# Wide matmuls for the high weights: one 512-column product over both parts of x, the halves added on eviction

## The chip, the cores and the metric

The kernel runs on one core of a Trainium2 chip. The metric is the device time of one execution in microseconds (us). It is told as the median of the timed runs. A profile of one execution with its trace goes with them.

The engines are called as in the profile: PE is TensorE's matmuls, PEld its weight loads, DVE is VectorE, ACT is ScalarE, POOL is GpSimd, SP is SyncE, which issues the DMAs.

## The reference, cut to what matters

256 tokens of 1024 features go through three layers. The first two are an mLSTM mixer and a gated spatial mixer, each followed by a feed-forward with a squared ReLU. The third is attention beside a convolution, then "PEER" experts, then a gated projection. Only two pieces of it matter here:

```python
y = jnp.square(jax.nn.relu(h @ ffn_w1[i])) @ ffn_w2[i]     # twice; w1 is 1024 x 4096

u = expert_u[et]                                           # peer: 16384 experts,
v = expert_v[et]                                           # 128 chosen per token
act = jax.nn.gelu(jnp.einsum('tnd,td->tn', u, xt)) * gt
return jnp.einsum('tn,tnd->td', act, v)
```

All of it is fp32, with seeded random inputs.

## The kernel before, in words

**Split products.** Every dense product is made of three matmuls in the fp32r type. ACT rounds an operand to a high part (`hi`, line 350, a cast), and DVE subtracts to get the rest (`lo`, line 351). The product is then hi times hi, hi times lo and lo times hi, summed in PSUM. Weights come in tiles of 1 MB (128 partitions x 2048 values). `weights` loads one and splits it into two tiles of 128x1024; the pool `wsp` has 4 buffers of `hi` and 4 of `lo`, so the cast for a tile reuses the buffer of the tile four places earlier and waits until PE has read that.

**Two forms of product.** In `dense_b` (line 392) the weights are the stationary operand and x, 256 tokens wide, is the moving one. One output tile is 128 outputs x 256 tokens and sums over k = 0 to 7, three matmuls of 256 columns for each k (`mm3`, lines 382 to 384): 24 matmuls and 24 weight loads. The tile lies in a PSUM buffer of the pool `mm`, which has two. In `Acc.emit` (line 113) x is stationary and the weights move, 512 columns in one matmul.

**Feed-forwards.** `ffn` (line 549) runs 16 steps n2. Each makes two tiles of the hidden layer with `pair`, which calls `dense_b`, except that the first tiles were already made ahead (`head`: 4 in the first feed-forward, 3 in the second). A tile is evicted by ACT (relu, line 565) and DVE (`s`, line 567, which reads PSUM and the relu), split into `h` and `l`, and one step later multiplied with `ffn_w2` in 24 matmuls of line 113. Between the steps `pump` lets side work run, here the conditioning rows `ada` (line 507, on DVE).

**Experts.** All 16384 experts are computed for all tokens in four quarters. `up(g)` (line 1142) makes the 32 tiles of a quarter in 16 steps b2 of two, each evicted by one ACT instruction (gelu, line 1147) from PSUM into `gx[g]`. `down(g)` multiplies `gx[g]` with the second matrix. The weight of an expert for a token is put in by `gate` (line 1150) in 32 steps of eight tokens for a set of quarters: DVE makes one-hot matrices `A`, `E` and `B` (lines 1159, 1161, 1164), PE multiplies them into a tile `sd` (line 1169 or 1180), and DVE multiplies `gx` with it. For quarter 0 (`wide`) ACT copies half of `sd` to `gs` (line 1171), DVE adds the other half (line 1172) and multiplies (line 1174); for the others DVE does it at once (line 1183). These steps are side work, taken from a budget after each step b2. The order is: route, gate(0) in the background of up(0), up(1), up(2); gate(1, 2) in the background of down(0), up(3); gate(3) in the background of down(1), down(2); down(3).

```python
            up(2, 3.0)
            self.drain()
            self.side = [gate((1, 2), iota2, op)]
            down(0, vp, 2.0)
            up(3, 4.0)
```

The budgets let two gate steps run per step b2 in up(2) and in up(3). Within each engine the instructions stand in a fixed order, which is set when the program is built; each engine works through its own in that order and waits on semaphores.

Of the kernel before, what the change touches and what calls it, by code (L numbers as in the profile page):

```python
# [10 lines left out]
F32 = mybir.dt.float32  # L11
F32R = mybir.dt.float32r
# [5 lines left out]
ALU = mybir.AluOpType  # L18
# [242 lines left out]
class Net:  # L261
# [129 lines left out]

    def dense_b(self, x, w, kc=KD, m=128, ps=None):

        (xh, xl), (wh, wl) = x, w
        if ps is None:
            ps = self.mm_tile()[:m, :T]
        for k in range(kc):
            last = self.mm3(ps, wh[:, k], wl[:, k], xh[:, k], xl[:, k], k == 0, k == kc - 1)
        self.flush(last)
        return ps  # L400

    def acc_tiles(self, n=1024):

# [27 lines left out]

        return [(ap[i][:, :1024 * min(2, n - 2 * i)], min(2, n - 2 * i), 128) for i in range((n + 1) // 2)]

    def pair(self, x, ap, i, first=0):

        have = min(2, max(0, len(self.head.ps) - first - 2 * i))
        ws = self.weights_b(ap[i][:, 1024 * have:]) if have < 2 else []
        for j in range(2):
            yield self.head.ps[first + 2 * i + j] if j < have else self.dense_b(x, ws[j - have])

    def h_tiles(self):
        return (self.hp.tile([128, KD, T], F32R, tag="hhi", name="hhi"),
                self.hp.tile([128, KD, T], F32R, tag="hlo", name="hlo"))

    def transpose_split(self, hi, lo, src, kc):

# [102 lines left out]
    def ffn(self, x, i, fin, pump=0.0):  # L549
        nc = self.nc  # L550
        w1, w2 = self.a["ffn_w1"], self.a["ffn_w2"]
        acc = Acc(self, 32, tail=6, fin=fin)
        with self.tc.tile_pool(name="ffn", bufs=6) as fp:
            pend = []

            def second():
                n2, parts = pend.pop(0)
                for p, w in zip(parts, self.weights(w2[i, n2])):
                    acc.add(p, w)

            for n2 in range(16):
                parts = []
                for ps in self.pair(x, w1[i], n2):
                    r = fp.tile([128, T], F32, tag="r", name="r", bufs=2)
                    nc.scalar.activation(r, ps, AF.Relu)
                    s = fp.tile([128, T], F32, tag="s", name="s", bufs=2)
                    nc.vector.scalar_tensor_tensor(s, ps, 0.0, r, op0=ALU.max, op1=ALU.mult)
                    h = fp.tile([128, T], F32R, tag="h", name="h")
                    l = fp.tile([128, T], F32R, tag="l", name="l")
                    self.split(h, l, s)  # L570
                    parts.append((h, l))
                pend.append((n2, parts))
                if 1 <= n2 < 14:
                    second()
                if 2 <= n2 < 13:
                    self.pump(pump)
                if n2 == 13:
                    self.drain()
            while pend:
                second()  # L580
        return fin.x
# [548 lines left out]
    def experts(self, x):  # L1130
        nc, a = self.nc, self.a
        with ExitStack() as es:
# [9 lines left out]
            def up(g, budget=0.0):  # L1142
                gx[g] = pools.get(g, gxa).tile([128, 32, T], F32, tag="gx", name="gx")
                for b2 in range(16):
                    for j, w in enumerate(self.weights_b(a["peer_u"][g * 16 + b2])):
                        ps = self.dense_b(x, w)
                        self.last = nc.scalar.activation(gx[g][:, 2 * b2 + j], ps, AF.Gelu_apprx_tanh)
                    self.pump(budget)

            def gate(groups, iota2, op, wide=False):  # L1150
# [4 lines left out]
                for t8 in range(T // 8):  # L1155
# [10 lines left out]
                    def apply_wide(ts=ts, A=A, B=B):  # L1166
                        pg = self.sd_tile().rearrange("p (t c j) -> p t c j", t=8, c=2)
                        for i in range(8):
                            nc.tensor.matmul(pg[:, i], A[:, i // 2, :, i % 2], B[:, :, i // 2, :, i % 2], start=True, stop=True)
                        s = op.tile([128, 8, 32], F32, tag="gs", name="gs")  # L1170
                        nc.scalar.copy(s, pg[:, :, 1])
                        nc.vector.tensor_tensor(s, s, pg[:, :, 0], op=ALU.add)
                        o = gx[groups[0]][:, :, ts]
# [332 lines left out]
```

## Time and profile before

| | |
|---|---|
| median of 3 timed runs | 1779.6 us (1777.91 to 1779.66) |
| the profiled execution: own time | 1777.44 us |
| its span in the trace | 1775.7 us |
| PE busy | 1727.9 us, 97% of the span, 11986 matmuls |
| PEld busy | 1545.4 us, 87% |
| DVE busy | 1370.4 us, 77% |
| ACT busy | 865.8 us, 49% |
| chain that ended last | PE 85%, DVE 7%, ACT 3%, DMA 2%, issue 2% |
| granted TensorE clock | 0.994 of full speed in the mean |
| moved by DMA | 352.51 MB, 199 GB/s in the mean |

The span runs from the first to the last instruction in the trace; the execution's own time has 1.7 us more around it. A matmul's busy time overlaps the next one's, so what a matmul costs in a stream is read from the distance of starts and not from its duration; the same holds, less strongly, for DVE and ACT. The shares are means over stages with different limits: the feed-forwards lie at about 176 to 365 us and 536 to 716 us of the span, up(0) to up(2) at about 975 to 1266, down(0) to 1362, up(3) to 1463, and the other down stages after it.

### The profile page before, as it was taken

What the parts mean: (1) busy time and instruction counts of PE and PEld (TensorE: products, weight loads), DVE (VectorE), ACT (ScalarE), POOL (GpSimd) and SP (SyncE); (2) the same over time, 40 slices, a digit from 0 to 9 for tenths busy, and PEclk for the clock granted to TensorE, in tenths of its full rate; (3) what the DMA queues carried; (4) which work ended last, traced back from release to release, by engine and by line L of the source; (5) the groups of instructions that cost most, each with busy time, mean ns of one, the idle gap of its engine ahead of it and who ended that gap; (6) DMA issues with size and microseconds to landing.
All of it is one profiled execution on the core that took longest, in us unless ns stands there. A gap on an engine that the chain in (4) does not pass through costs nothing.

```text
span 1775.7 us, 29680 instructions
## 1 busy us (share of the span) xinstructions
PE 1727.9 (97%) x11986; PEld 1545.4 (87%) x11986; DVE 1370.4 (77%) x2366; ACT 865.8 (49%) x1372; POOL 42.8 (2%) x50
## 2 busy tenths in 40 slices
PE   7999999999999999998999999999999999999998
PEld 3878889887879899898989999999988998888886
DVE  6687887579957655899867999789788958965654
ACT  3565445454545544564645445455444344444644
POOL 0110000000000000002000000000000000000000
PEclk9999999999999999999999999999999999999999
DMA  9874897467827653543436555544555454455751
GB/s 350 307 273 155 326 332 279 165 244 258 292 70 287 240 189 117 197 143 119 146 119 227 175 178 182 184 164 170 172 180 175 147 187 167 167 179 180 264 190 48
DMA packets 59604, 352.51 MB, mean 199 GB/s; under 512 B 6165, under 2 KB 12613, under 8 KB 19273
## 3 DMA queue, kind: packets, MB, share of 16 engines
q1 hardware_dynamic: 59466, 350.61, 56.1%
q8 instruction: 94, 1.54, 0.3%
q14 instruction: 44, 0.36, 0.1%
HBM read 349.51 MB, written 1.07 MB: 197 GB/s over the span
## 4 chain that ended last, share of the span: by engine, by line
PE 85%; DVE 7%; ACT 3%; DMA 2%; issue 2%; POOL 1%; SPq 0%; POOLq 0%; DVEq 0%; ACTq 0%
PE acc L113 38%; PE mm L382 13%; PE mm L384 13%; PE mm L383 13%; PE head L135 2%; DVE lo L351 2%; PE sd L1180 2%; DMA st<-in_ada_w_dram 1%; ACT hi L350 1%; DVE yc L894 1%; ACT junk L162 1%; DMA st<-in_a_w_v_dram 1%; DVE ada L507 1%; POOL rs_r L427 1%; PE sd L799 1%
## 5 line engine op out<-in xcount | busy, mean ns | idle before, releaser
L351 DVE TENSOR_TENSOR lo<-st,hi 128x1024 fp32r<-128x1024 f32 (+1 forms) x507 | 614.8, 1225 | 176.4 <-ACT hi L350 175.1
L350 ACT CAST hi<-st 128x1024 fp32r<-128x1024 f32 (+1 forms) x507 | 523.7, 1048 | 453.1 <-PE mm L383 225.2
L382 PE MATMUL mm<-hhi,hi 128*128 128x256 f32 (+1 forms) x2000 | 575.8, 288 | 0.7 <-ACT qz L629 0.7
L384 PE MATMUL mm<-hhi,lo 128*128 128x256 f32 (+1 forms) x2000 | 566.9, 284 | 8.0 <-DVE lo L351 7.9
L383 PE MATMUL mm<-hlo,hi 128*128 128x256 f32 (+1 forms) x2000 | 567.0, 284 | 0.0
L384 PEld LDWEIGHTS mm<-hhi,lo 128*128 128x128 f32 (+1 forms) x2000 | 383.7, 192 | 9.0 <-DVE lo L351 9.0
L382 PEld LDWEIGHTS mm<-hhi,hi 128*128 128x128 f32 (+1 forms) x2000 | 384.0, 192 | 3.6 <-issue 1.4
L383 PEld LDWEIGHTS mm<-hlo,hi 128*128 128x128 f32 (+1 forms) x2000 | 384.3, 192 | 3.1 <-issue 2.1
L113 PE MATMUL acc<-hi,vh 128*128 128x512 f32 x448 | 141.0, 396 | 0.0
L113 PE MATMUL acc<-lo,vh 128*128 128x512 f32 x448 | 138.3, 390 | 0.0
L113 PE MATMUL acc<-hi,vl 128*128 128x512 f32 x448 | 137.9, 389 | 0.0
L507 DVE SCALAR_TENSOR_TENSOR ada<-st,cact,ada 128x1024 f32<-128x1024 f32 x74 | 95.2, 1287 | 10.1 <-DMA st<-in_ada_w_dram 5.9
L113 PE MATMUL acc<-hi,h 128*128 128x512 f32 x320 | 100.5, 395 | 2.4 <-ACT hi L350 2.4
L113 PE MATMUL acc<-lo,h 128*128 128x512 f32 x320 | 100.4, 394 | 0.1
L113 PE MATMUL acc<-hi,l 128*128 128x512 f32 x320 | 99.9, 393 | 0.0
L113 PEld LDWEIGHTS acc<-hi,vl 128*128 128x128 f32 x448 | 84.1, 188 | 17.9
L113 PEld LDWEIGHTS acc<-lo,vh 128*128 128x128 f32 x448 | 84.1, 188 | 17.9
L113 PEld LDWEIGHTS acc<-hi,vh 128*128 128x128 f32 x448 | 81.6, 188 | 15.0
L350 ACT CAST vh<-gx 128x512 fp32r<-128x512 f32 x64 | 39.9, 624 | 96.2 <-PE acc L113 94.1
L113 PE MATMUL acc<-hi,hhi 128*128 128x512 f32 x224 | 73.6, 406 | 4.0 <-ACT hhi L350 2.1
L113 PE MATMUL acc<-lo,hhi 128*128 128x512 f32 x224 | 72.4, 396 | 1.0 <-DVE lo L351 0.9
L113 PEld LDWEIGHTS acc<-lo,h 128*128 128x128 f32 x320 | 60.3, 189 | 13.7 <-DVE lo L351 1.0
(380 smaller groups left out, 2174.8 us busy)
## 6 DMA issues: line engine op xcount, KB each, us to landing
st<-in_peer_u_dram SPq DMA_DIRECT2D x64, 1024.0 KB, 4.8
st<-in_peer_v_dram SPq DMA_DIRECT2D x64, 1024.0 KB, 4.8
st<-in_ffn_w_dram SPq DMA_DIRECT2D x63, 1024.0 KB, 4.9
st<-in_ada_w_dram SPq DMA_DIRECT2D x40, 1024.0 KB, 5.6
st<-in_ada_w_dram SPq DMA_DIRECT2D x16, 512.0 KB, 7.2
st<-in_b_w_u_dram SPq DMA_DIRECT2D x8, 1024.0 KB, 5.0
st<-in_b_w_v_dram SPq DMA_DIRECT2D x8, 1024.0 KB, 4.8
st<-in_b_w_out_dram SPq DMA_DIRECT2D x8, 1024.0 KB, 5.8
```

The source lines that it names most:

```text
L113: ins = mm(self.t[t][j], a[:, ts], b[:, j * 512:(j + 1) * 512], start=first and a is xh and b is wh, stop=last and a is xl)
L135: net.nc.tensor.matmul(ps[:, t * 128:(t + 1) * 128], w[:, k], x(k), start=k == 0, stop=k == KD - 1)
L162: nc.scalar.activation(net.junk[:, halves[h]], src, AF.Square, scale=1.0 / 32.0, accum_out=out[:, h:h + 1])
L350: i = self.nc.scalar.copy(hi, src)
L351: return i.ins, self.nc.vector.tensor_tensor(lo, src, hi.bitcast(F32), op=ALU.subtract).ins
L382: mm(out, ahi, bhi, start=start, stop=False)
L383: mm(out, ahi, blo, start=False, stop=False)
L384: return mm(out, alo, bhi, start=False, stop=stop)
L427: nc.gpsimd.tensor_tensor(r, v, m, op=ALU.pow)
L507: nc.vector.scalar_tensor_tensor(s, w, c, s, op0=ALU.mult, op1=ALU.add)
L799: nc.tensor.matmul(ps[:, t], v[:, t, n * 128:(n + 1) * 128], ws[:, n], start=False, stop=t == 1)
L1180: nc.tensor.matmul(pg[:, i], A[:, i // 2, :, i % 2], B[:, c, i // 2, :, i % 2], start=c == 0, stop=c == 1)
```

## The change

For the 57 hidden tiles of the feed-forwards that are not made ahead, and for the 64 tiles of up(2) and up(3), a new `dense_w` takes the place of `dense_b`. The two parts of x now lie side by side in one tile `h2` (`h_tiles`), so that one matmul of 512 columns multiplies the high weights with both. Each k has this one and a matmul of 256 columns for the low weights: 16 matmuls per tile where there were 24. The result fills a whole PSUM buffer of 512 columns, and its two halves must be added: `added` has ACT copy the second half to SBUF (`half`) and DVE add the first half to it. In the feed-forwards DVE then squares in a further instruction. In the experts the sum is written to `gx` and ACT's gelu runs on it in place.

```diff
     def dense_b(self, x, w, kc=KD, m=128, ps=None):
-        (xh, xl), (wh, wl) = x, w
+        xh, xl, (wh, wl) = x[0], x[1], w
...
+    def dense_w(self, x, w):
+
+        xh, x2, (wh, wl) = x[0], x[2], w
+        mm = self.nc.tensor.matmul
+        ps = self.mm_tile()
+        for k in range(KD):
+            first, last = k == 0, k == KD - 1
+            if last:
+                mm(ps[:, :T], wl[:, k], xh[:, k], start=False, stop=False)
+            i = mm(ps, wh[:, k], x2[:, k], start=first, stop=last)
+            if not last:
+                i = mm(ps[:, :T], wl[:, k], xh[:, k], start=False, stop=False)
+        self.flush(i)
+        return ps
+
+    def added(self, ps, out, pool, tag):
+
+        c = pool.tile([128, T], F32, tag=tag, name="half", bufs=2)
+        self.nc.scalar.copy(c, ps[:, T:])
+        self.nc.vector.tensor_tensor(out, ps[:, :T], c, op=ALU.add)
...
-    def pair(self, x, ap, i, first=0):
+    def pair(self, x, ap, i, first=0, wide=False):
...
-            yield self.head.ps[first + 2 * i + j] if j < have else self.dense_b(x, ws[j - have])
+            yield self.head.ps[first + 2 * i + j] if j < have else (self.dense_w if wide else self.dense_b)(x, ws[j - have])
 
     def h_tiles(self):
-        return (self.hp.tile([128, KD, T], F32R, tag="hhi", name="hhi"),
-                self.hp.tile([128, KD, T], F32R, tag="hlo", name="hlo"))
+
+        x = self.hp.tile([128, KD, 2, T], F32R, tag="h2", name="h2")
+        return x[:, :, 0], x[:, :, 1], x.rearrange("p k c t -> p k (c t)")
...
-                for ps in self.pair(x, w1[i], n2):
-                    r = fp.tile([128, T], F32, tag="r", name="r", bufs=2)
-                    nc.scalar.activation(r, ps, AF.Relu)
+                for ps in self.pair(x, w1[i], n2, wide=True):
                     s = fp.tile([128, T], F32, tag="s", name="s", bufs=2)
-                    nc.vector.scalar_tensor_tensor(s, ps, 0.0, r, op0=ALU.max, op1=ALU.mult)
+                    if ps.shape[1] == T:
+
+                        r = fp.tile([128, T], F32, tag="r", name="r", bufs=2)
+                        nc.scalar.activation(r, ps, AF.Relu)
+                        nc.vector.scalar_tensor_tensor(s, ps, 0.0, r, op0=ALU.max, op1=ALU.mult)
+                    else:
+                        self.added(ps, s, fp, "r")
+                        nc.vector.scalar_tensor_tensor(s, s, 0.0, s, op0=ALU.max, op1=ALU.mult)
...
-                        ps = self.dense_b(x, w)
-                        self.last = nc.scalar.activation(gx[g][:, 2 * b2 + j], ps, AF.Gelu_apprx_tanh)
+                        o = gx[g][:, 2 * b2 + j]
+                        if g < 2:
+                            ps = self.dense_b(x, w)
+                        else:
+
+                            ps = o
+                            self.added(self.dense_w(x, w), o, op, "gs")
+                        self.last = nc.scalar.activation(o, ps, AF.Gelu_apprx_tanh)
...
-                        s = op.tile([128, 8, 32], F32, tag="gs", name="gs")
+                        s = op.tile([128, T], F32, tag="gs", name="gs").rearrange("p (t j) -> p t j", t=8)
```

Where the new instructions stand in the engines' orders is shown at three places.

The first is DVE in the middle of up(2), one step b2 with its two gate steps. `lo` is the split of weights, `A`, `E`, `B`, `gs` and `gx<-gx,gs` are the gate's. Before:

```order
L1161 TENSOR_TENSOR E<-iota_8916,rT_8904 128x4x64 x2
L351 TENSOR_TENSOR lo<-st,hi 128x1024 x2
L1159 TENSOR_TENSOR A<-iota_8916,rT_8903 128x1024
L1164 TENSOR_TENSOR B<-E,gT 128x8x64
L1172 TENSOR_TENSOR gs<-gs,sd 128x256 x2
L1174 TENSOR_TENSOR gx<-gx,gs 128x32x8 x2
L1159 TENSOR_TENSOR A<-iota_8916,rT_8903 128x1024
L1164 TENSOR_TENSOR B<-E,gT 128x8x64
```

The same step with the change (lines are 33 further down):

```order
L1194 TENSOR_TENSOR E<-iota_8509,rT_8497 128x4x64 x2
L351 TENSOR_TENSOR lo<-st,hi 128x1024 x2
L1192 TENSOR_TENSOR A<-iota_8509,rT_8496 128x1024
L1197 TENSOR_TENSOR B<-E,gT 128x8x64
L1192 TENSOR_TENSOR A<-iota_8509,rT_8496 128x1024
L1205 TENSOR_TENSOR gs<-gs,sd 128x256 x2
L1207 TENSOR_TENSOR gx<-gx,gs 128x32x8 x2
L1197 TENSOR_TENSOR B<-E,gT 128x8x64
L421 TENSOR_TENSOR gx<-mm,half 128x256 x2
```

The two adds (line 421) stand together at the end of the step, behind the whole gate work of it.

The second is ACT at the end of up(2), after the last full pair of gate steps, with buffer numbers. `hi_12811` is the cast that reuses the buffer which the tile `mm_12713` reads; `half` are the new copies.

```order
L350 CAST hi_12807<-st_12805 128x1024
L1204 COPY gs_12692<-sd_12683 128x256
L1204 COPY gs_12705<-sd_12696 128x256
L350 CAST hi_12811<-st_12805 128x1024
L420 COPY half_12709<-mm_12666 128x256
L420 COPY half_12730<-mm_12713 128x256
```

The copy for `mm_12666` stands behind a cast that waits for the end of the next tile, `mm_12713`.

The third is PE in up(3), with buffer numbers, at the sixth of its steps b2.

```order
L411 MATMUL mm_14400<-h2_8438,hi_14392 128x512
L411 MATMUL mm_14459<-h2_8438,hi_14396 128x512
L413 MATMUL mm_14400<-h2_8438,lo_14393 128x256
L411 MATMUL mm_14400<-h2_8438,hi_14392 128x512
L413 MATMUL mm_14400<-h2_8438,lo_14393 128x256
```

The first matmul of the tile `mm_14459` now stands inside `mm_14400`, ahead of the matmuls that need `lo_14393`; it happens again two steps later. Outside the changed stages the order of PE, DVE, ACT and POOL is as before, and on SP one load changes places with its neighbours.

## Rows read from the trace of the kernel before

**Rows 1.** The page's first line.

```profile
span 1775.7 us, 29680 instructions
```

**Rows 2.** Chain that ended last, second feed-forward: start us, us, what.

```profile
570.90 5.47 PE acc L113 x24
582.12 5.47 PE acc L113 x24
```

**Rows 3.** Groups of instructions: count, busy, mean ns | idle, releaser.

```profile
L565 ACT ACTIVATE r<-mm 128x256 f32<-128x256 f32 x57 | 21.6, 380 | 47.6 <-PE mm L384 47.6
L1147 ACT ACTIVATE gx<-mm 128x256 f32<-128x256 f32 x128 | 48.7, 380 | 0.0
```

**Rows 4.** Busy time by stretch: us, PE, PEld, DVE, ACT, POOL, PEclk, DMA, GB/s.

```profile
187.00:330.00 143.00, 140.58 (x866) 125.02 (x866) 114.52 (x135) 70.94 (x101) 2.01 (x1) 0.99 0.81 298
536.00:705.00 169.00, 168.94 (x1059) 152.55 (x1058) 109.46 (x137) 82.44 (x127) 1.08 (x2) 1.00 0.60 214
1180.00:1240.00 60.00, 60.00 (x615) 59.57 (x615) 60.00 (x113) 30.39 (x58) 0.00 (x0) 1.00 0.47 159
1380.00:1412.00 32.00, 32.00 (x362) 31.83 (x360) 31.83 (x57) 11.98 (x18) 0.00 (x0) 1.00 0.47 163
```

**Rows 5.** Chain that ended last, a DVE chain on SBUF of 256 columns.

```profile
738.20 3.67 DVE yc L894 x10
```

**Rows 6.** Timeline of PE in the first feed-forward, around its longest wait.

```profile
198.27 0.28 PE L384 MATMUL mm<-hhi,lo 128*128 128x256 f32 x1
200.92 1.21 PE L113 MATMUL acc<-hi,h 128*128 128x512 f32 x4 [2.37 <-ACT hi L350]
...
203.18 1.06 PE L113 MATMUL acc<-hi,l 128*128 128x512 f32 x2
204.03 1.06 PE L113 MATMUL acc<-lo,h 128*128 128x512 f32 x2
```

**Rows 7.** Timeline of DVE in up(2), one step: start us, us, what.

```profile
1192.65 2.35 DVE L351 TENSOR_TENSOR lo<-st,hi 128x1024 fp32r<-128x1024 f32 x2
1194.92 0.68 DVE L1159 TENSOR_TENSOR A<-iota,rT 128x1024 f16<-128x1024 f16 x1
1195.52 0.42 DVE L1164 TENSOR_TENSOR B<-E,gT 128x512 f16<-128x512 f16 x1
1195.88 0.75 DVE L1172 TENSOR_TENSOR gs<-gs,sd 128x256 f32<-128x256 f32 x2
1196.54 1.17 DVE L1174 TENSOR_TENSOR gx<-gx,gs 128x256 f32<-128x256 f32 x2
1197.63 0.69 DVE L1159 TENSOR_TENSOR A<-iota,rT 128x1024 f16<-128x1024 f16 x1
1198.22 0.43 DVE L1164 TENSOR_TENSOR B<-E,gT 128x512 f16<-128x512 f16 x1
1198.56 0.50 DVE L1161 TENSOR_TENSOR E<-iota,rT 128x256 f16<-128x256 f16 x2
1198.96 2.36 DVE L351 TENSOR_TENSOR lo<-st,hi 128x1024 fp32r<-128x1024 f32 x2
```

**Rows 8.** Timeline of PE in up(2): the gate's matmuls between two of the tiles'.

```profile
1181.62 0.28 PE L384 MATMUL mm<-hhi,lo 128*128 128x256 f32 x1
1181.75 0.66 PE L1169 MATMUL sd<-B,A 128*128 128x64 f16 x16
1182.24 0.36 PE L382 MATMUL mm<-hhi,hi 128*128 128x256 f32 x1
```

**Rows 9.** Timeline of ACT in up(2).

```profile
1194.52 1.05 ACT L350 CAST hi<-st 128x1024 fp32r<-128x1024 f32 x1 [1.54 <-issue]
1195.48 0.64 ACT L1171 COPY gs<-sd 128x256 f32<-128x256 f32 x2
```

**Rows 10.** Timeline of DVE in up(3), the same instruction one step apart.

```profile
1385.54 1.41 DVE L1183 TENSOR_TENSOR gx<-gx,sd 128x256 f32<-128x256 f32 x4
1392.34 1.42 DVE L1183 TENSOR_TENSOR gx<-gx,sd 128x256 f32<-128x256 f32 x4
```

## The prediction

> **What bounds the kernel now.** I set the sum against the profiled execution: 1777.4 us, of which the span is 1775.7 [rows 1]. It lies 2.2 us below the median of 1779.6, so a time worked out here is raised by 2.2 at the end. No change, as far as a measurement of this kernel can tell, means within 0.2%, 3.55 us either way.
>
> First the chain that ended last: PE is 85% of it, so look at what a matmul costs in a stream. In the second feed-forward 24 matmuls of 512 columns stand in 5.47 us, 228 ns each. From one such group to the next are 11.22 us; the other 5.75 hold the 48 matmuls of 256 columns of two hidden tiles, 119.8 ns each [rows 2]. Twice the columns are not twice the time: at 2.4 GHz 256 columns are 106.7 ns and 512 are 213.3, so each matmul carries some 13 to 14 ns beyond its columns.
>
> Second the groups, for what ACT does per tile now: relu or gelu, 380 ns [rows 3].
>
> Third the busy time by stretch, which says who has room. In the feed-forwards PE fills nearly all of the time and DVE 114.5 of 143 us and 109.5 of 169. In the middle of up(2) PE and DVE are both busy for 60.00 of 60 us, in up(3) DVE for 31.83 of 32 [rows 4]. There any new DVE work meets an engine with no gap.
>
> **The saving on PE.** Per k, three matmuls of 256 columns (3 x 120 = 360 ns) become one of 512 and one of 256 (227 + 120 = 347): 13 ns, eight times per tile, 0.106 us. That is 57 x 0.106 = 6.1 us in the feed-forwards, 32 x 0.106 = 3.4 in each of up(2) and up(3), 12.9 in all if PE sets the pace everywhere.
>
> Beside that row the Trainium skill ("TensorE: Matmul & The Clock Gate", section "Wait — 56ns, not 53.3ns?") speaks against the change: it gives a fixed cost of only about 2.5 ns per matmul at the higher clock. By it the 968 matmuls that vanish would save an estimated 2.4 us. The rows disagree, with five times that.
>
> **Feed-forwards.** ACT's copy takes the place of its relu, both of 128x256 from PSUM, so ACT gains nothing [rows 3]. DVE gets one more instruction per tile, the square on SBUF. Ten dependent DVE instructions of 256 columns take 3.67 us, 0.37 each [rows 5], so 28 and 29 tiles add some 10.5 us each: 125 of 143 and 120 of 169 us [rows 4], which still fits. Per step a tile has two turns of 2.75 us before its buffer is needed; copy, add and square together take 1.1. So I cost these at nothing, covered by PE's own stream; without that cover each tile would pay about 0.37. What stays is the saving, 6.1 us, less where something else already ends the wait: in the first feed-forward PE waits 2.37 us for a cast of weights that come by DMA (the share of the DMA engines is 0.81 there), and faster matmuls only lengthen such a wait [rows 4, 6]. I take **-5.5**. Bounds: -6.1, and -2.3 if a third of the tiles lose it.
>
> **up(2).** One step b2 lies between two splits of weights, 1192.65 and 1198.96: 6.31 us, filled by DVE instruction to instruction [rows 7]. PE needs in it 48 x 0.12 = 5.76, and between two tile matmuls 0.62 us for the gate's 16, 0.50 above the normal distance [rows 8]: 6.26. The two engines are level. The change adds two adds of 256 columns from PSUM. The nearest row is the gate's own add of that form, two in 0.66 us start to start [rows 7]. So DVE needs 6.31 + 0.67 = 7.0 us and PE 6.26 - 0.21 = 6.05 to 6.1. PE has two buffers; the adds stand at the end of the step behind the whole gate work, so the tile after next waits there, 0.9 us per step. Twelve steps carry two gate steps. Through their order I get a first wait of 0.8, ten of 0.9, and at the end one longer: the copy for `mm_12666` stands behind the cast into the buffer that `mm_12713` reads. So that tile ends, then cast 1.05 [rows 9], split 1.17 (half of 2.35) and add 0.33 [rows 7], 2.6 us. Together 12.4, less 16 x 0.21 = 3.4 for PE's saving: **+9.0**. ACT is busy for 30 of 60 us [rows 4], so two copies of 0.32 [rows 9] and a gelu on SBUF cost nothing themselves. Bounds: if the split of the next weights and E fill some of the waits, DVE alone sets 11 steps of 0.66 more against 5 of saving, +6.2; above, the hand-overs between copy, add and matmul add about 0.1 per step, +10.
>
> **up(3).** Here a step lasts 6.80 us [rows 10], of which PE's matmuls fill all and DVE all but a little [rows 4]. After the change DVE needs 6.68 + 0.67 = 7.35 and PE 6.80 - 0.21 = 6.59: 0.75 short in each of the seven steps with two gate steps, 5.3 us. DVE's lead over PE at the start takes 0.7 of it. The remaining 4.6 should show as three waits of about 0.9, 1.5 and 2.2, where the first matmul of a tile (`mm_14459`) now stands inside the tile ahead and holds the rest of that up. Less 3.4: **+1.2**. Bounds -1 and +4.
>
> **The clock.** After the idle 2.37 us at 198.5 us the 512-column matmuls stand 0.43 us apart instead of 0.23, which is 1.2 in place of 2.4 GHz [rows 6]. The half rate lasts some 3.4 us and so costs 1.7. The waits of 2.6 and 2.2 us that I expect at the end of up(2) and in up(3) are near 2.37; those of 0.9 are not. I count one such stretch, **+1.7**; bounds none and three.
>
> **Sum**: -5.5 + 9.0 + 1.2 + 1.7 = +6.4, 1783.8 against the own time of 1777.4, and 1786.0 against the median.
>
> **Rivals.**
>
> *The adds cancel the gain.* The floor in up(2) (+6.2), up(3) at -1, the full saving in the feed-forwards (-6.1) and no further drop of the clock: -0.9, 1778.7. For it speaks that DVE's instructions could be set closer once PE waits; against it that rows 7 show no gap to close. Chance 0.2.
>
> *PE sets the pace everywhere, faster.* If DVE found 0.86 us per step in up(2), the 0.66 of the adds and the 0.21 that PE gains, all 121 tiles keep their saving: -12.9, 1766.7. It decides at that point, and the 60.00 of 60 speak against it [rows 4]; shorter DVE instructions while PE idles would speak for it. Chance 0.08.
>
> *It is dearer.* If the `ada` rows on DVE in the feed-forwards leave no room for the square in their steps, some 15 of the 28 steps lose their 0.21 (3.2 us), and if two more waits end at half clock (3.4), the sum is +13.0, 1792.6. The DVE share of 80% in the first feed-forward allows it, but it is a mean [rows 4]. Chance 0.12.
>
> *The merge saves almost nothing on PE.* If a matmul of 512 columns right beside one of 256 paid its weight load in full, so that the pair took 358 instead of 347 ns, the saving would shrink to a fifth, +10.4 on the sum, about 1797. In rows 2 the streams of 512 and 256 are each unmixed, so this isn't excluded, but no row speaks for it. Chance 0.02. The skill's 2.5 ns, named above, would give a similar time.
>
> **How the numbers follow.** Forecast, slower: 0.58, itself within 1783 to 1790 (feed-forwards -6.1 to -4, up(2) +8 to +10, up(3) 0 to +3, up to two stretches at half clock). Cancel 0.20, faster 0.08, dearer 0.12, no saving 0.02. The likeliest gives 1786.0. The range runs from 1778.0 (the cancel case in) to 1791.5 (half of the dearer case in); outside stay 0.08 + 0.02 + some 0.09 of the edges. Faster by over 0.2% is only the case of PE's pace, 0.08. Within 0.2%, up to 1783.2, is the cancel case and the lowest edge of the forecast, 0.22. Slower is the rest, 0.70.
>
> **What would show it.** In the feed-forwards the steps should shorten from 11.22 to about 11.0 us, with a 512-256 pair in 347 ns. In up(2) the steps with two gate steps should lengthen from 6.31 to about 7.0, with DVE full and PE waiting once per step for DVE's add; its other four steps shorten by 0.2. up(3) should hold two or three waits behind the add and the split. If PE's waits in up(2) are of another releaser, or if DVE's step stays at 6.3, the step that prices the adds is wrong. If the pair is not 347 ns, the saving is.

## The result and the profile after

The change made the kernel slower: 1798.2 us (1795.9 to 1799.7, 4 runs) against 1779.5 (1777.9 to 1779.7, 4 runs), a ratio of 1.0108, 95% interval [1.0093, 1.0122]. Forecast were 1786.0 and a range up to 1791.5. The sign was right, the size three times too small, and the time lies outside the range.

The page's first line; that of before is [rows 1].

```profile
span 1795.6 us, 27876 instructions
```

**Where the time went.** Both kernels make the same 716 casts to a high part on ACT, in nearly the same order, so the start of the same cast tells how far the one runs behind the other. From such marks (us of the span of before, and how much later the same cast starts after):

| cast of before starts at | 178 | 362 | 536 | 715 | 1014 | 1173 | 1287 | 1362 | 1468 | 1755 |
|---|---|---|---|---|---|---|---|---|---|---|
| after, later by | +2.7 | +0.9 | -0.6 | -2.7 | -1.9 | -1.8 | +15.5 | +15.5 | +19.6 | +19.6 |

The first feed-forward gained 1.8 us, the second 2.1, up(2) lost 17.3 and up(3) 4.1. The 1.5 us between the feed-forwards are a stretch at half clock that only the profile of before has there (granted clock 0.50 from 526.5 to 529.9 us). The 2.7 us ahead of the first feed-forward are taken up below. The busy time by stretch shows what changed in each; its columns are as in [rows 4], and so are its stretches:

```profile
187.00:330.00 143.00, 139.96 (x686) 116.08 (x685) 122.96 (x160) 71.05 (x101) 2.01 (x1) 0.99 0.82 305
536.00:705.00 169.00, 168.94 (x845) 142.33 (x845) 122.03 (x169) 85.30 (x130) 1.08 (x2) 1.00 0.61 213
1180.00:1240.00 60.00, 51.44 (x385) 42.72 (x384) 56.16 (x113) 31.25 (x64) 0.00 (x0) 1.00 0.42 141
1380.00:1412.00 32.00, 31.26 (x294) 26.78 (x292) 30.19 (x62) 16.30 (x30) 0.00 (x0) 1.00 0.39 133
```

The third row decides. In the middle of up(2) PE was busy for 60.00 of 60 us, and so was DVE. Now **neither** is full: PE 51.44, DVE 56.16. Two engines that both have idle time may be waiting for each other, and the timelines show that these do. The timeline of DVE over one step b2 shows the one half of it (start us, us, what, in brackets the idle time before and what ended it; [rows 7] is the same stretch before):

```profile
1196.68 0.69 DVE L1192 TENSOR_TENSOR A<-iota,rT 128x1024 f16<-128x1024 f16 x1 [0.49 <-PE sd L1202]
1197.29 0.42 DVE L1197 TENSOR_TENSOR B<-E,gT 128x512 f16<-128x512 f16 x1
1197.63 0.68 DVE L1192 TENSOR_TENSOR A<-iota,rT 128x1024 f16<-128x1024 f16 x1
1198.23 0.74 DVE L1205 TENSOR_TENSOR gs<-gs,sd 128x256 f32<-128x256 f32 x2
1198.89 1.15 DVE L1207 TENSOR_TENSOR gx<-gx,gs 128x256 f32<-128x256 f32 x2
1199.95 0.42 DVE L1197 TENSOR_TENSOR B<-E,gT 128x512 f16<-128x512 f16 x1
1200.28 0.76 DVE L421 TENSOR_TENSOR gx<-mm,half 128x256 f32<-128x256 f32 x2
1200.95 0.49 DVE L1194 TENSOR_TENSOR E<-iota,rT 128x256 f16<-128x256 f16 x2
1201.35 2.36 DVE L351 TENSOR_TENSOR lo<-st,hi 128x1024 fp32r<-128x1024 f32 x2
1204.21 0.69 DVE L1192 TENSOR_TENSOR A<-iota,rT 128x1024 f16<-128x1024 f16 x1 [0.50 <-PE sd L1202]
```

From A to A are 7.53 us, where it was 6.31. The two adds (L421) take their 0.67 us, as priced, and DVE's work is 7.0, as priced. But 0.5 us of idle time has come in, ahead of A, which waits for PE's matmuls of the gate. PE's timeline in the same stretch shows the other half:

```profile
1193.33 0.47 PE L411 MATMUL mm<-h,hi 128*128 128x512 f32 x1 [1.09 <-DVE gx L421]
...
1196.23 0.66 PE L1202 MATMUL sd<-B,A 128*128 128x64 f16 x16
...
1200.86 0.47 PE L411 MATMUL mm<-h,hi 128*128 128x512 f32 x1 [1.06 <-DVE gx L421]
```

It is a closed loop. The add releases a PSUM buffer, and PE starts a tile at 1193.33. Behind that tile stand the gate's 16 matmuls, done at about 1196.7. They free the buffer that A is written to, so A starts at 1196.68. Behind A stand B, A, gs, gx and B, 3.60 us, and only then the next add at 1200.28, which lets PE go on at 1200.86. PE's part is 3.35 us, DVE's 3.60, the add with its hand-over to PE 0.58: 7.53. The two splits and E (L351, L1194) lie beside PE's part; that they cost nothing is tested below.

The copies on ACT are tied to the same place. `half` takes its buffers from those of the gate's `gs`, so ACT can copy only when DVE's multiplication has freed one:

```profile
1199.55 0.37 ACT L420 COPY half<-mm 128x256 f32<-128x256 f32 x1 [1.54 <-DVE gx L1207]
```

No run separates this tie from the place of the add on DVE.

PE's waits between 1160 and 1270 us, from the table of waits (what waited for what: us, times, longest):

```profile
PE mm L411 <- DVE gx L421: 14.8, 13, 2.8
```

The longest, at the end of up(2), was forecast. The copy stands on ACT behind a cast that waits for PE, and PE comes back at half clock (1.2 GHz): the granted clock is 0.51 in the mean from 1262.20 to 1265.70 us, and from one matmul of 512 columns to the next are 0.65 us where it is otherwise 0.35. ACT first, then PE:

```profile
1259.96 1.04 ACT L350 CAST hi<-st 128x1024 fp32r<-128x1024 f32 x1 [1.78 <-PE mm L411]
1260.91 0.64 ACT L420 COPY half<-mm 128x256 f32<-128x256 f32 x2
```

```profile
1262.75 0.77 PE L411 MATMUL mm<-h,hi 128*128 128x512 f32 x1 [2.82 <-DVE gx L421]
...
1263.52 0.63 PE L411 MATMUL mm<-h,hi 128*128 128x512 f32 x1
...
1264.17 0.63 PE L411 MATMUL mm<-h,hi 128*128 128x512 f32 x1
```

In up(3) PE waits in the two places that the order showed, each time for the add and then for the split behind it:

```profile
1411.52 0.50 PE L411 MATMUL mm<-h,hi 128*128 128x512 f32 x1 [0.74 <-DVE gx L421]
...
1413.25 0.39 PE L413 MATMUL mm<-h,lo 128*128 128x256 f32 x1 [1.24 <-DVE lo L351]
...
1433.99 0.50 PE L411 MATMUL mm<-h,hi 128*128 128x512 f32 x1 [0.74 <-DVE gx L421]
...
1435.46 0.39 PE L413 MATMUL mm<-h,lo 128*128 128x256 f32 x1 [0.96 <-DVE lo L351]
```

The idle time in brackets counts from the end of a matmul's busy time, which reaches into the next matmul's; by starts, these four places are 4.5 us longer than the same places without a wait. Behind the second pair the clock is at half, as the busy time of this stretch shows (PEclk 0.50, columns as in [rows 4]); behind the first, which idles longer, it is not.

```profile
1436.30:1439.70 3.40, 3.40 (x13) 2.71 (x12) 3.11 (x3) 0.00 (x0) 0.00 (x0) 0.50 0.44 108
```

In the feed-forwards the chain that ended last has one of these pieces per pair of tiles (start us, us, what); [rows 2] are those of before:

```profile
569.89 5.45 PE acc L113 x24
...
580.97 5.45 PE acc L113 x24
```

The step is 11.08 us instead of 11.22. It was to fall by 0.21 and fell by 0.14, 0.07 per tile; ten of the thirteen steps between 540 and 700 us have just these two lengths.

### The profile page after: what moved, and what is told of

It reads as the page before. It is cut to its first block, busy times and chain, and to the rows that moved or that the text cites. A ratio compares the mean times of both kernels' runs of the same rounds, so it can differ in the third digit from the quotient of the medians.

```text
span 1795.6 us, 27876 instructions
## 1 busy us (share of the span) xinstructions
PE 1727.1 (96%) x11018; PEld 1493.4 (83%) x11018; DVE 1413.2 (79%) x2487; ACT 889.2 (50%) x1436; POOL 43.3 (2%) x50
## 4 chain that ended last, share of the span: by engine, by line
PE 81%; DVE 11%; ACT 3%; issue 2%; DMA 2%; POOL 1%; SPq 0%; DVEq 0%; ACTq 0%; POOLq 0%
PE acc L113 37%; PE mm L411 11%; PE mm L384 6%; PE mm L382 6%; PE mm L383 6%; PE mm L413 5%; DVE lo L351 2%; PE head L135 2%; PE sd L1213 1%; DVE ada L529 1%; ACT hi L350 1%; DVE A L1192 1%; DVE yc L921 1%; PE mm L410 1%; PE sd L503 1%
## 5 line engine op out<-in xcount | busy, mean ns | idle before, releaser
L351 DVE TENSOR_TENSOR lo<-st,hi 128x1024 fp32r<-128x1024 f32 (+1 forms) x507 | 613.9, 1223 | 136.8 <-ACT hi L350 132.4
L411 PE MATMUL mm<-h,hi 128*128 128x512 f32 x968 | 350.0, 404 | 16.4 <-DVE gx L421 16.3
L384 PE MATMUL mm<-h,lo 128*128 128x256 f32 (+1 forms) x1032 | 292.9, 284 | 7.8 <-DVE lo L351 7.8
L382 PE MATMUL mm<-h,hi 128*128 128x256 f32 (+1 forms) x1032 | 297.0, 288 | 0.7 <-ACT qz L656 0.7
L383 PE MATMUL mm<-h,hi 128*128 128x256 f32 (+1 forms) x1032 | 292.7, 284 | 0.0
L413 PE MATMUL mm<-h,lo 128*128 128x256 f32 x847 | 238.8, 282 | 2.2 <-DVE lo L351 2.2
L113 PE MATMUL acc<-hi,h 128*128 128x512 f32 x768 | 232.0, 398 | 6.9 <-ACT hi L350 4.8
L411 PEld LDWEIGHTS mm<-h,hi 128*128 128x128 f32 x968 | 179.6, 189 | 56.6 <-issue 19.2
L384 PEld LDWEIGHTS mm<-h,lo 128*128 128x128 f32 (+1 forms) x1032 | 197.8, 192 | 8.9 <-DVE lo L351 8.8
L382 PEld LDWEIGHTS mm<-h,hi 128*128 128x128 f32 (+1 forms) x1032 | 198.0, 192 | 1.2 <-ACT qz L656 0.9
L383 PEld LDWEIGHTS mm<-h,hi 128*128 128x128 f32 (+1 forms) x1032 | 198.1, 192 | 0.8 <-issue 0.6
L113 PEld LDWEIGHTS acc<-hi,h 128*128 128x128 f32 x768 | 142.2, 188 | 39.1 <-ACT hi L350 6.7
L413 PEld LDWEIGHTS mm<-h,lo 128*128 128x128 f32 x847 | 161.2, 190 | 7.2 <-DVE lo L351 2.8
```

The source lines that it names most:

```text
L113: ins = mm(self.t[t][j], a[:, ts], b[:, j * 512:(j + 1) * 512], start=first and a is xh and b is wh, stop=last and a is xl)
L351: return i.ins, self.nc.vector.tensor_tensor(lo, src, hi.bitcast(F32), op=ALU.subtract).ins
L382: mm(out, ahi, bhi, start=start, stop=False)
L383: mm(out, ahi, blo, start=False, stop=False)
L384: return mm(out, alo, bhi, start=False, stop=stop)
L411: i = mm(ps, wh[:, k], x2[:, k], start=first, stop=last)
```

## The experiments

All times are medians. The kernel before ran beside each group of runs on the same chip, at 1778.7, 1778.7, 1778.3 and 1779.5 us.

### One part alone

**The feed-forwards alone**: the experts as before.

```diff
-                        if g < 2:
+                        if g < 4:
```

> Wide matmuls in the feed-forwards only; the experts as before. The traces of before and after differ by some -2.2 us over the first feed-forward, -3.6 over the second, and by +2.7 us in the first 60 us, ahead of any wide matmul. If the feed-forwards' gain is real and the early 2.7 us is a difference between executions, the time is 5 to 6 us below before, about 1774. Rival: the new layout of x (both parts in one tile) costs the 2.7 us at the start in every run; then about 1776.5.

Measured: 1777.7 us, ratio 0.9996 [0.9984, 1.0008], no difference that can be told, and above both expectations. By the marks the first feed-forward gains 1.9 us and the second 2.1, and then 1.9 us go again between 715 and 1014 us. That stage starts 2.0 us earlier but gets its weights, which come by DMA, hardly earlier. This cast on ACT waits 1.92 us for them, and starts 0.67 us earlier than the same cast before (723.02 us, with a wait of 0.55):

```profile
722.35 2.00 ACT L350 CAST hi<-st 128x1024 fp32r<-128x1024 f32 x2 [1.92 <-DMA st<-in_w_qi_dram]
```

Three stretches at half clock (granted clock 0.50) fall into that stage in this profile, two in the profile of before. So the saving on PE is there, and the end of the program hardly sees it.

**The layout alone**: both parts of x in one tile, three matmuls of 256 columns everywhere.

```diff
-                        if g < 2:
+                        if g < 4:
...
-                for ps in self.pair(x, w1[i], n2, wide=True):
+                for ps in self.pair(x, w1[i], n2):
```

> The layout of the change alone: both parts of x in one tile, but three matmuls of 256 columns everywhere, as before. All four runs with this layout have their first 60 us 2.3 to 4.3 us longer than the profile of before. If the layout costs this, the time is 2 to 3 us above before, about 1781, and the feed-forwards' saving was there but paid for at the start. If it was the profile of before that was quick at its start, the time is that of before within 1 us.

Measured: 1778.0 us, ratio 0.9998 [0.9989, 1.0007]. The layout costs nothing by the time at the end. Its profile too is 1.9 us behind that of before at 178 us, and level from 1014 us on. All fifteen profiles of the other kernels that the marks cover, each with this layout, are 0.8 to 4.3 us behind there. That the one profiled execution of before had a quick start is the likely reading, but with one profile of that layout it is not shown.

**No copy and no add in the experts**: gelu reads the first half of the buffer.

```diff
-                            ps = o
-                            self.added(self.dense_w(x, w), o, op, "gs")
+                            ps = self.dense_w(x, w)[:, :T]
```

> The change without copy and add in the experts: gelu reads the first half of the PSUM tile, and the second half (the product with the low part of x) is left out. If the add on DVE is the whole cause, up(2) and up(3) are each 3.4 us shorter than before (PE's saving, uncovered), and the time is 1779.5 - 5.8 - 6.8 = 1767, or 1769.5 with the early 2.7 us. Rival (the mixed stream of 512 and 256 columns, or the full PSUM buffer, costs time itself): up(2) stays at its old length or longer, and the time stays above 1773.

Measured: 1775.9 us, ratio 0.9981 [0.9967, 0.9995]. The time lies on the rival's side of 1773, but not by the rival's cause: PE waits nowhere in up(2), where the marks show 2.7 us less than before, and 2.3 less in up(3). That is 5.0 us of the 6.8 expected there; the rest of the distance to 1767 lies ahead of up(2), which this profile reaches 3.3 us behind that of before. So the wide matmuls cost nothing by themselves, and all that up(2) and up(3) lose comes with the copy and the add. But the saving is 0.07 to 0.08 us per tile here too, not 0.106.

### What closes the loop in up(2)

**Four buffers of A and B** in up(2), in place of two.

```diff
-                    A = op.tile([128, 4, 128, 2], F16, tag="A", name="A")
+                    ap = self.ex or op
+                    ap = ap if t8 % 2 else op
+                    A = ap.tile([128, 4, 128, 2], F16, tag="A", name="A")
...
+            with self.tc.tile_pool(name="ohx", bufs=2) as self.ex:
+                up(2, 3.0)
+                self.drain()
```

> The change, with four buffers of A and B for the gate steps that run in up(2) in place of two; the order of DVE's instructions is the same. Theory (a loop between the engines): a step of 7.53 us is PE's 3.4 us from the first matmul released by the add to the gate's matmuls, then DVE's 3.6 us from A, which waits for these matmuls to free its buffer, to the add. With more buffers DVE's wait of 0.5 us before A goes, the step is DVE's own 7.0 us, PE waits some 0.6 us in place of 1.1, and the time falls by 5 to 6.5 us, to about 1792. Rival (DVE's amount of work, or its slowness, sets the step): step stays at 7.5, time stays at 1798.

In this run the pool of down(0)'s tiles is also opened only behind up(2).

Measured: 1804.1 us, ratio 1.0149 [1.0128, 1.0169]: no gain, and 6 us above the change, where neither theory had it. The timeline of DVE shows the same wait, once per step of 7.52 us:

```profile
1199.32 0.69 DVE L1194 TENSOR_TENSOR A<-iota,rT 128x1024 f16<-128x1024 f16 x1 [0.50 <-PE sd L1204]
...
1206.84 0.69 DVE L1194 TENSOR_TENSOR A<-iota,rT 128x1024 f16<-128x1024 f16 x1 [0.50 <-PE sd L1204]
```

A still waits for the gate's matmuls: it was put a whole step further ahead of its use, to where the fourth buffer is just being read. More buffers were used to run ahead, not to wait less. So this run tested nothing of the loop. By the marks 2.8 of the 6 us are in up(2), at whose end the wait of 2.82 us comes twice (at 1257.94 and 1268.76 us), each with a stretch at half clock. The other 3 lie ahead of up(2), where this kernel does what the change does, and stay unexplained.

**A, E and B behind the last add**, with the four buffers.

```diff
+                    with self.tc.issue_after(self.plus.ins) if self.ex else ExitStack():
```

> The change, with four buffers of A and B in up(2) and with the gate's A, E and B put behind the last add on DVE, so that no instruction of DVE waits for the gate's matmuls of the same step to free a buffer (the run with four buffers alone kept this wait, as A moved one step forward with them). Theory (the loop between DVE and PE is closed by A's wait): DVE is full, the step falls from 7.53 to about 7.0 us, PE's wait from 1.1 to 0.6 to 0.9, the time by 5 to 6.5 us to about 1792. Rival (the loop is closed by the adds behind the gate's multiplications, whatever A does): 7.5 us stay, about 1798, and only putting the adds ahead helps, as that run did.

Measured: 1837.4 us, ratio 1.0341 [1.0321, 1.036]: far worse, by neither theory. A no longer waits, but now the add is preceded on DVE, and the copy on ACT, by the split and the cast of the next weights, whose buffer PE frees at the end of a tile. That is the pattern that the change has once, at the end of up(2); here it comes in every step. PE's timeline:

```profile
1199.96 0.77 PE L411 MATMUL mm<-h,hi 128*128 128x512 f32 x1 [2.82 <-DVE gx L421]
...
1210.75 0.76 PE L411 MATMUL mm<-h,hi 128*128 128x512 f32 x1 [2.82 <-DVE gx L421]
```

DVE's, at the split ahead of the add:

```profile
1205.63 1.22 DVE L351 TENSOR_TENSOR lo<-st,hi 128x1024 fp32r<-128x1024 f32 x1 [3.08 <-ACT hi L350]
```

The step is 10.8 us. Between 1170 and 1300 us the trace has twelve such waits of 2.82 us and twelve stretches with a granted clock of 0.50. What stands ahead of the add decides, and a wait ahead of it that leads back to PE closes the loop.

**Copy and add ahead of the gate's multiplications.**

```diff
-        self.flush(i)
+        self.end = i
         return ps
...
         self.nc.vector.tensor_tensor(out, ps[:, :T], c, op=ALU.add)
+        self.flush(self.end)
```

> The change, with the copy and the add of a tile written ahead of the gate's multiplications, so that DVE's two adds no longer stand together at the end of the step, but one ahead and one behind. Theory (a loop through the adds' place): PE is released earlier, the loop no longer closes over the whole gate work, DVE's 7.0 us of work sets the step, and the time falls by 5 to 8 us, to 1790 to 1793, with PE's waits shorter and split over the two tiles. Rival (DVE's amount sets it, and 7.5 is what it takes): no change, 1798.

Measured: 1787.1 us, ratio 1.0042 [1.0029, 1.0056], 11 us below the change and 3 below the forecast. In up(2) the marks show +3.6 us in place of +17.3. Most steps have no wait of PE at all; once in some five steps PE has to wait for DVE, which then is really behind:

```profile
1195.79 0.66 PE L1203 MATMUL sd<-B,A 128*128 128x64 f16 x16
1201.94 0.66 PE L1203 MATMUL sd<-B,A 128*128 128x64 f16 x16
...
1207.87 0.50 PE L411 MATMUL mm<-h,hi 128*128 128x512 f32 x1 [1.58 <-DVE gx L421]
1209.00 0.38 PE L413 MATMUL mm<-h,lo 128*128 128x256 f32 x1 [0.63 <-DVE lo L351]
1211.66 0.66 PE L1203 MATMUL sd<-B,A 128*128 128x64 f16 x16
```

Steps of 6.15 us and one of 9.72 (from one group of the gate's matmuls to the next). up(3), where the same edit left the order's two places as they are, keeps its +4.1.

**One split less per step**, outside the loop: in up(2) the low part of every second tile's weights is left out.

```diff
-                at = self.split(hi, lo, st[:, j:j + w])
+                if one and j:
+                    at = self.nc.scalar.copy(hi, st[:, j:j + w]).ins, self.lo
+                    lo = hi
+                else:
+                    at = self.split(hi, lo, st[:, j:j + w])
```

> The change, but in up(2) the low part of every second tile's weights is left out (its matmuls take the high part in its place), so that DVE has one split of 1.13 us less per step; the order of all else on DVE is the same. The split lies beside PE's tiles, outside the loop from the add over PE's tiles, the gate's matmuls, A, B, A, gs, gx, B to the next add. Theory (that loop sets the step): the step stays at 7.5 us, DVE's wait ahead of A grows from 0.5 to 1.6 us, the time stays within 2 us of the change's 1798. Rival (DVE's amount sets the step): the step falls by 1.1 to 6.4 us, and the time by 12 to 13 us to 1785.

Measured: 1799.2 us, ratio 1.0113 [1.0099, 1.0128], the time of the change. DVE has 1.13 us less to do in every step and the step stays at 7.53; all that it gains becomes idle time. DVE, then PE:

```profile
1200.28 0.69 DVE L1196 TENSOR_TENSOR A<-iota,rT 128x1024 f16<-128x1024 f16 x1 [1.59 <-PE sd L1206]
...
1207.81 0.69 DVE L1196 TENSOR_TENSOR A<-iota,rT 128x1024 f16<-128x1024 f16 x1 [1.63 <-PE sd L1206]
```

```profile
1196.96 0.47 PE L415 MATMUL mm<-h,hi 128*128 128x512 f32 x1 [1.06 <-DVE gx L425]
1204.45 0.47 PE L415 MATMUL mm<-h,hi 128*128 128x512 f32 x1 [1.06 <-DVE gx L425]
```

PE's waits in these steps, 1.06 to 1.11 us, are those of the change. This settles it: the loop sets the step, not DVE's amount of work, which is what the prediction had added up.

### Spreading the gate's work

**One gate step per step b2** in up(2) (two in its first three) and in up(3), two in up(1).

```diff
-                    self.pump(budget)
+                    self.pump(budget(b2) if callable(budget) else budget)
...
-                up(1, 2.6)
+                up(1, 2.8)
...
-            up(2, 3.0)
+            up(2, lambda b: 2.8 if b < 3 else 2.6)
...
-            up(3, 4.0)
+            up(3, 2.0)
```

> The change, with the gate's steps spread: two per step b2 in up(1), one in up(2) but for its first three, one in all 16 steps of up(3) in place of two in eight. Theory (what up(2) and up(3) lose is DVE work bunched in steps with two gate steps): DVE needs some 5.1 us per step with one, PE 5.8, no tile waits for an add, and up(2) and up(3) keep PE's saving of 3.4 us each: 17.4 + 4.1 + 6.8 = 28 us below the change's 1798, about 1770. Rival (an add behind the gate's work holds PE up with one gate step too): PE waits for the add once in each step, and the time stays at 1776 or above.

Measured: 1791.7 us, ratio 1.008 [1.0066, 1.0093], where 1770 was expected. The rival was right. With half the gate work a step of up(2) still takes 6.33 us, where PE's matmuls need 5.9. DVE's waits from 1200 to 1265 us:

```profile
DVE A L1192 <- PE sd L1202: 6.2, 10, 0.6
DVE lo L351 <- ACT hi L350: 5.9, 10, 0.6
```

DVE idles 1.2 us per step and PE still waits for its add: the add stands behind A and behind a split, which both wait for PE, the split by way of ACT's cast.

**The same, with copy and add ahead** (the two edits together).

```diff
-        self.flush(i)
+        self.end = i
...
+        self.flush(self.end)
...
+            up(2, lambda b: 2.8 if b < 3 else 2.6)
```

> The gate's steps spread as in the run before, and the copy and add written ahead of the gate's multiplications. Theory: with spread gate steps the adds' place decides nothing, about 1770 as in that run, within 1.5 us. Rival (the adds' place): 3 us or more below that run.

Measured: 1782.7 us, ratio 1.0024 [1.0014, 1.0034], 9 us below the run before it; the rival again. Now steps of up(2) take 5.94 us and those of up(3) 6.19, without waits inside the stages. What is left is lost at their ends: 2.0 us by starts at the end of up(3), and more at the end of up(2), where the gate's last multiplication has become late for down(0):

```profile
1268.16 0.95 PE L113 MATMUL acc<-hi,vh 128*128 128x512 f32 x2 [4.54 <-ACT vh L350]
```

**The gate ended earlier**: two gate steps in the first six steps of up(2) and the first three of up(3).

```diff
+            up(2, lambda b: 2.8 if b < 6 else 2.6)
...
+            up(3, lambda b: 3.0 if b < 3 else 2.0)
```

> Gate steps spread, adds ahead of the gate's multiplications, and the gate's work ended some three steps b2 before the ends of up(2) and up(3). The run before it with spread gate steps and adds ahead had steps of 5.94 us in up(2), but lost 4.5 us and a stretch at half clock at its end and 2.0 us at the end of up(3), where the first split of down waits for the gate's last multiplication. Theory (what is left of the loss stands at these two ends): 4.5 + 1.7 + 2.0 less, some 6 to 8 us below that run's 1782.7: 1775 to 1777, 2 to 4 us below before. Rival (the adds cost PE elsewhere): 1780 or more.

Measured: 1777.7 us, ratio 0.9995 [0.9984, 1.0006]. That is just above the forecast. Both ends are repaired; two waits of PE (2.0 and 1.1 us between starts) remain in the doubled steps of up(2).

Three runs vary this. **Without the wide form in the feed-forwards**:

```diff
-                for ps in self.pair(x, w1[i], n2, wide=True):
+                for ps in self.pair(x, w1[i], n2):
```

> The same without the wide matmuls in the feed-forwards. If the feed-forwards' saving reaches the end, this run is 4 to 5 us slower than the run with them; if the stages behind them (casts and splits of weights that come by DMA, stretches at half clock) take it back, as the run with the feed-forwards alone suggests (1.0 us below before), it is within 1.5 us of that run.

Measured: 1779.8 us, ratio 1.0011 [1.0, 1.0021]: 2.1 us slower than with it, between the two expectations. **With the wide form in up(0) and up(1) too**:

```diff
-                        if g < 2:
+                        if g < 0:
```

> The same as the first, with the wide form in up(0) and up(1) too. If DVE has room beside the routing, another 3.4 us each are saved, 1768 to 1771; if the routing's long DVE chains hold the adds up, as the gate's work does in up(2), PE waits for the add in many steps of up(0), and the time is above the first run's.

Measured: 1790.5 us, ratio 1.0064 [1.0048, 1.0081]. The marks lose 12 us between 1014 and 1173, in up(0) and up(1). PE's waits from 1015 to 1175 us, from the table of waits, are again for the add and for splits behind it:

```profile
PE mm L413 <- DVE lo L351: 5.6, 9, 1.2
PE mm L411 <- DVE gx L421: 2.2, 4, 1.1
```

**Spread gate steps without any wide matmul**, the control:

```diff
-                        if g < 2:
+                        if g < 4:
...
-                for ps in self.pair(x, w1[i], n2, wide=True):
+                for ps in self.pair(x, w1[i], n2):
```

> Control: the gate's steps spread as in the first run, and no wide matmul anywhere (the layout of x stays). If spreading by itself is worth nothing, since PE and DVE are level in up(2) as it is, the time is that of before within 1.5 us, 1777 to 1780, and the first run's gain is that of the wide form. If spreading is itself a gain, it is below 1777.

Measured: 1779.3 us, ratio 1.0005 [0.9996, 1.0013]. Spreading by itself is worth nothing: by the marks it loses 1.5 us in up(1) and gains 1.5 in up(2). This is the control of the spreading with two gate steps in the first six steps of up(2); the alternating order that follows has no control of its own.

**Double gate steps alternating with single ones** in up(2).

```diff
+            up(2, lambda b: 2.8 if b < 12 and b % 2 == 0 else 2.6)
```

> As the run with spread gate steps, adds ahead and the gate ended early, but in up(2) the six steps b2 with two gate steps alternate with steps of one, in place of standing together. Theory (PE's waits of 2.0 and 1.1 us in the doubled stretch of that run come from DVE falling behind over several such steps): they go, up(2) ends some 3 us earlier, time 1774 to 1775.5. Rival (the wait comes from the order within one such step): the waits stay, 1777 to 1778.

Measured: **1774.9 us, ratio 0.9979 [0.9969, 0.9988]**, 4.6 us faster than before by the medians, 2.1 to 5.5 by the interval: the only order of the whole change that beats it, and as forecast. The profiled execution took 1770.3 us, the shortest of the ten, so its marks show more than the medians. PE waits nowhere in up(2), and both engines are full again (columns as in [rows 4]):

```profile
1180.00:1240.00 60.00, 60.00 (x439) 52.04 (x439) 59.99 (x115) 38.60 (x75) 0.00 (x0) 1.00 0.52 176
```

up(1) and up(2) together are 2.4 us shorter than before, up(3) 1.8.

**Wide in the feed-forwards and up(3) alone**, with up(3)'s gate steps spread and the adds ahead.

```diff
-                        if g < 2:
+                        if g < 3:
...
-            up(3, 4.0)
+            up(3, lambda b: 3.0 if b < 3 else 2.0)
```

> Wide in the feed-forwards and in up(3) alone, with spread gate steps in up(3) and adds ahead; up(0) to up(2) as before. From the stages of the runs so far: up(3) 2.0 to 2.5 us less than before, up(2) as before, the feed-forwards some 1 to 2 less: 1775 to 1776. Rival (each of these gains is taken back by the next stage): 1778 to 1779, no change.

Measured: 1776.0 us, ratio 0.998 [0.9971, 0.9989]. As forecast. By the marks up(3) gains 1.8 us and the feed-forwards 3.8, which this time are kept.

## Why the prediction was wrong

The prediction failed at up(2), whose cost it took from two sums of work where the waits form a loop: +17.3 us instead of +9.0. Second to that, the saving per tile was put at 0.106 us and is 0.07.

- **What bounds the kernel**: right. PE paces it, and up(2) is where DVE and PE are level. But DVE did not stay full there, as the prediction expected; it is busy for 56.16 of 60 us.
- **The saving on PE** was mis-sized. The step of two tiles fell by 0.14 us, not 0.21: 0.07 per tile, 8.5 us over 121 tiles and not 12.9. What failed is the sum 227 + 120 = 347. It took both distances from unmixed streams [rows 2]. In the mixed one a matmul of 512 columns stands 234.7 ns ahead of the next of 256 (mean of 195 in the second feed-forward) and that one 116.9 ahead of the next of 512 (mean of 168): 351.6. Against three of 119.8 that is 7.8 ns for each k, 0.062 us per tile; the group of 24 matmuls behind, 5.45 us for 5.47, gives the other 0.01. The rival of no saving, whose place was just this, had 358: the pair lies two fifths of the way to it. The Trainium skill's 2.5 ns per matmul ("TensorE: Matmul & The Clock Gate", section "Wait — 56ns, not 53.3ns?") is still well below what this trace shows: 0.07 us for eight removed matmuls is 8.75 ns each.
- **Feed-forwards**, -5.5: the marks show -1.8 and -2.1, or 3.9, and 0.07 x 57 = 4.0 follows from the smaller saving. The square on DVE was hidden, as said. The bound of -2.3 does not follow from its condition: a third of the tiles without their 0.106 leaves -4.1. But the run with the feed-forwards alone kept only 1.0 us of the gain, within its interval of none; with the saving in the experts, the comparison of two runs gives 2.1.
- **up(2)**, +9.0: this is the step that failed. "So DVE needs 7.0 us and PE 6.05 to 6.1 ... the tile after next waits there, 0.9 us per step" compares two sums of work and takes the larger. The adds and DVE's 7.0 us were right. But the waits form a loop with a length of its own, 7.53 us, and the loop exceeds both sums. All its parts but the hand-over from the add to PE were in the rows of before: about 3.3 us of PE (a tile of 2.8, the gate's matmuls 0.50 [rows 8]), then A, B, A, gs, gx, B, 3.6 us between starts [rows 7], then the add. Eleven steps grew by 1.19 us each instead of 0.69, which is 5.6 of the 8.3 us by which up(2) was missed. The last step with gate work grew by 4.2 instead of 2.4, about 1.5 of it the half clock, which the sum had counted apart. The other four steps were to give 0.8 and gave nothing.
- The wait at the **end of up(2)** came as forecast, 2.82 for 2.6 us, with its cause.
- **up(3)**, +1.2 within -1 and +4: +4.1, of which one stretch at half clock, granted from 1436.3 to 1439.7 us, is 1.7. The places and causes of the waits were right, and so was their sum: 4.5 us by starts for 4.6, though in four waits and not three. The saving was 2.2 (32 x 0.07) instead of 3.4. These three give 4.0 of the 4.1.
- **The clock**, +1.7 for one stretch in up(2) and up(3): two, one behind the wait of 2.82 us and one behind up(3)'s second pair of waits. That the length of the idle time tells where one comes, as the prediction reasoned, is not borne out: the first pair in up(3) idles 1.98 us and no stretch follows, the second 1.70.
- **The rivals**: "the adds cancel the gain" and "PE sets the pace everywhere" were wrong for this order. The best order (1774.9) goes towards the second, and it needed two things: room on DVE, which this rival named, by moving gate steps out of up(2), and the adds ahead of the gate's multiplications. Room alone gave 1791.7, the place alone 1787.1, both 1782.7; the rest came from ending the gate's work earlier and alternating its steps. "The merge saves almost nothing" named the nearest time, 1797, but by luck: it left up(2) at the forecast's price and took the whole miss for the saving, which is short by 4.4 us.

## What to carry to other kernels

When an instruction is added to an engine that is level with another, don't stop at the two sums of work: follow the waits around, from the added instruction to what it releases on the other engine, to what that one releases back, to what stands in program order ahead of the added instruction again, and add up that loop. Try an eviction that frees a scarce buffer ahead of all work of its engine that waits for the engine which needs that buffer; here it gave 11 us. More buffers for a waiting instruction did not help here, as the order ran further ahead with them.

## What the runs showed that was not expected

- A DVE split of 1.13 us taken out of every step of up(2) with two gate steps changed nothing at all: 1799.2 against 1798.2 us, PE's wait 1.06 us in both.
- The same adds in other places of the order: 1837.4 us behind the next split (with four buffers, and the gate's A, E and B moved behind them), 1798.2 in the change, 1787.1 ahead of the gate's multiplications. What stands ahead of an instruction of 0.33 us was worth up to 50 us.
- A matmul of 512 columns followed by one of 256 takes 234.7 ns to the next start, 8 ns more than in a stream of 512 alone (227), and the 256 that follows 3 ns less than in its own (119.8).
